# Token lists of all experts from one set of products, GpSimd's weight splits begun later, the second expert's transposes moved

## The chip, the cores and the metric

The kernel runs on one core of a Trainium2 chip. The metric is the device time of one execution in microseconds (us). The engines are TensorE (PE, matrix products, with PEld for its weight loads), VectorE (DVE), ScalarE (ACT), GpSimd (POOL), and SyncE (SP), which issues most DMAs. GpSimd issues the DMAs that gather and scatter rows by a list of indices.

## The reference, cut to what matters

The model has two layers on 512 tokens of width 1024. Each layer is a token mixer and then a mixture of 16 experts. The change lies in the expert part:

```python
g_prob = softmax(xt @ w_group + b_group);  g_val, g_idx = top_k(g_prob, 1)
e_logits = (xt @ w_expert + b_expert).reshape(N, 4, 4)      # only the chosen group's four count
e_val, e_idx = top_k(softmax(e_logits[chosen group]), 2);  e_val = e_val / sum(e_val)
gates = one_hot(g_idx * 4 + e_idx) * g_val * e_val          # two experts for each token
for e in range(16):
    hid = silu(xt @ w_gate[e]) * (xt @ w_up[e])             # 1024 -> 512
    out = out + gates[:, e:e + 1] * (hid @ w_down[e])       # 512 -> 1024
```

## The kernel before, in words

Tokens lie on 128 partitions in four tiles (`NT` = 4). Each layer first scores the tokens (`route_lt`), then `select` finds each token's group and its two best experts, in two halves of two tiles (`TS` = 2): comparisons into `beat` and `above`, the chosen group `og`, the mask `ab` of chosen experts, and a product `pk` of `ab` with a triangular matrix, which counts the earlier tokens of the same expert. `rk` (L873) is the token's place in that expert's list, or 0.

`moe` then works expert by expert on at most 96 tokens (`CAP`). `make_list(e)` (L1257) compares `rk` of expert e with the places 1 to 96 (`oneh`, L1259, DVE), and four PE matmuls with the token numbers (`pi`, L1263) give a column of 96 indices, which DVE stores (`first` L1276 for the first two experts, `lists` L1277 or L1266). GpSimd gathers the expert's rows by it (`xg`, L1278; two buffers, `XG` = 2). `gathered_t` transposes them on PE (`xt`, L521); ACT and DVE store them as a high and a low half (`th` L481, `tl` L482), since every product is made of three matmuls of halves (`mm3`, L475 to L477). `gate_up` makes `pg` and `pu`, ACT and DVE make `sg` = silu(`pg`)·`pu` (L1311, L1312), scaled by a number of `gx`; `hidden_t` transposes it (`ht`, then `hh`, `hl`); `down` makes the two halves of `pd`; ACT writes `yb` times the gate (L1343), and GpSimd scatters it with addition (`h_d` in the first layer, `out_dram` in the second, L1346). `pg` and `pu` share a PSUM tag of three buffers ("pj"), so `pu` of the second expert takes the buffer of the first expert's `pg`, which is free after the ACT step that reads it together with `gx`.

The gates take a way of their own: `rest` (L890 to L928) works out the gate values on DVE, `ga`, writes them to DRAM (`g_d`, L928), and GpSimd gathers them by each list (`gx`, L1351).

The weights of an expert are six units of 1 MB. Each comes by DMA into a `raw` buffer and is split in two pieces: ACT writes the high part (`wh`, L191), DVE or GpSimd the low one (`wl`, L193). Six pieces are held at a time. `add_moe` says whose work a low part is: GpSimd has one piece of every sixth unit (`i[0] % 6 == 3`) while the unit's number is under 60. With the order of the units (gate and up of an expert, then down of the expert before it) these are pieces of `up` for expert 0 and of `down` for the next ones. `ws.hold()` stops the weight DMAs ahead of the lists, and `ws.go` lets them on behind a mark on DVE.

The order on each engine is set by the tile framework's scheduler, from the recorded operations, their dependences and its own costs; `marks` and `behind` pin operations behind others of the same engine.

Of the kernel before, what the change touches and what calls it, by code (L numbers as in the profile page):

```python
# [15 lines left out]
F16 = mybir.dt.float16  # L16
# [8 lines left out]
P = 128  # L25
# [26 lines left out]
XG = 2  # L52
# [224 lines left out]
def tile_trunk(ctx: ExitStack, tc: tile.TileContext, x, a_norm, a_w_in, a_b_f, a_q_gain, a_k_gain, a_w_out,  # L277
# [64 lines left out]
    def add_moe(layer):  # L342
        i = [0]
        tags = RINGS[layer]

        def add4(w, r0, c0):
            ws.add([(cols(0, 512, 512), rows(w, r0, 4, c0, 512))],
                   [[(k * 1024, 1024, None, "pool" if i[0] < 60 and (i[0] % 6, k) == (3, 0) else None)] for k in range(2)],
                   tags[i[0] % len(tags)], "m")
            i[0] += 1  # L350

        def gu(e):
            for w in (moe_w_gate, moe_w_up):
                for half in range(2):
                    add4(w[layer, e], half * 512, 0)

        def down(e):
            for n in range(2):
                add4(moe_w_down[layer, e], 0, n * 512)

        gu(0)
        for e in range(1, NE):
            gu(e)
            down(e - 1)
        down(NE - 1)
# [472 lines left out]
    def select(layer, t0, t1):  # L838
# [3 lines left out]
        if t0 == 0:  # L842
            r.update(lg=kt([P, NT, 20], "lg"), beat=kt([P, NT * 5, 4, 4], "beat"),
                     above=kt([P, NT * 5, 4], "above"), og=kt([P, NT, 4], "og"), ab=kt([P, NT, NE], "ab", BF16),
                     rk=kt([P, NT, NE], "rk", F16))
        lg, ab = r["lg"], r["ab"]
# [20 lines left out]
        for t in range(t0, t1):  # L867
            o = pk[:, (t - t0) * 16:(t - t0) * 16 + 16]
            for u in range(t + 1):
# [3 lines left out]
        nc.vector.scalar_tensor_tensor(r["rk"][:, t0:t1], pk[:, 0:n * 16].rearrange("p (t e) -> p t e", e=NE), 1.0,  # L873
                                       ab[:, t0:t1], op0=ALU.add, op1=ALU.mult)

    def route(layer):
# [3 lines left out]
        lg, ab, og = r["lg"], r["ab"], r["og"]  # L880
# [10 lines left out]
        def rest():  # L891
# [7 lines left out]
            a12 = kt([P, 2, NT, NE], "a12")  # L899
            a5 = r["above"].rearrange("p (t r) e -> p t r e", r=5)  # L900
            for k in range(2):
                nc.vector.scalar_tensor_tensor(a12[:, k].rearrange("p t (g e) -> p t g e", e=4), a5[:, :, 1:5], float(k),
                                               og[:, :, :, None].to_broadcast([P, NT, 4, 4]),
                                               op0=ALU.is_equal, op1=ALU.mult)
# [330 lines left out]
    def moe(layer):  # L1235
        r = rt[layer]
        with ExitStack() as st:
# [19 lines left out]
            def make_list(e):  # L1257
                oneh = pm.tile([P, NT, CAP], F16, tag="oneh", name=f"oneh{e}", bufs=1)
                nc.vector.tensor_tensor(oneh, slot16[:, None, 0:CAP].to_broadcast([P, NT, CAP]),  # L1259
                                        rk[:, :, e:e + 1].to_broadcast([P, NT, CAP]), op=ALU.is_equal)  # L1260
                pi = ps("tr", f"pi{e}")[0:CAP]
                for t in range(NT):
                    nc.tensor.matmul(pi[:, 0:1], oneh[:, t, :], tok16[:, layer * NT + t:layer * NT + t + 1],  # L1263
                                     start=t == 0, stop=t == NT - 1)
                if e >= XG:
                    nc.vector.tensor_scalar_add(lists[:, e:e + 1], pi[:, 0:1], OOB)  # L1266
                li = lists[:, e:e + 1]
                if layer == 0 and e == NE - 1:
                    r["last"] = kt([CAP, NT], "last")
                    for t in range(NT):  # L1270

                        nc.vector.tensor_scalar(r["last"][:, t:t + 1], pi[:, 0:1], OOB + NT - t, 1.0 / NT,
                                                op0=ALU.add, op1=ALU.mult)
                if e < XG:
                    li = first[:, e:e + 1]
                    nc.vector.tensor_scalar(li, pi[:, 0:1], OOB, S - 1.0, op0=ALU.add, op1=ALU.min)  # L1276
                    nc.vector.tensor_scalar_add(lists[:, e:e + 1], pi[:, 0:1], OOB)  # L1277
                nc.gpsimd.indirect_dma_start(  # L1278
                    out=xg[e % XG], out_offset=None, in_=xn_d,
                    in_offset=bass.IndirectOffsetOnAxis(ap=li, axis=0), bounds_check=S - 1, oob_is_err=False)  # L1280
# [7 lines left out]
            def gate_up(e, th, tl):  # L1288
                pg, pu = ps("pj", f"pg{e}")[0:CAP], ps("pj", f"pu{e}")[0:CAP]
                for o in (pg, pu):  # L1290
# [12 lines left out]
                    for i in range(4):  # L1303
                        wh, wl = ws.get()
                        for j in range(2):
                            kc = i * 2 + j
                            c = slice(j * 512, j * 512 + 512)
                            mm3(o, th[:, kc, :], tl[:, kc, :], wh[:, c], wl[:, c], kc == 0, kc == KC - 1)
                sg = pm.tile([CAP, DE], F32, tag="sg", name=f"sg{e}", bufs=1)
# [45 lines left out]

            for i in range(XG):
                make_list(i)
                if i == 1:
                    ws.go(marks()[mybir.EngineType.DVE].name, last_unit[layer] + 1)
# [12 lines left out]
            make_list(2)  # L1372
# [4 lines left out]
            for e in range(NE):  # L1377
                sg = gate_up(e, *tt)
                if e + 1 < NE:
                    tt = gathered_t(e + 1)  # L1380
                if hprev is not None:
                    down(e - 1, *hprev)
                if e + 3 < NE:
                    make_list(e + 3)
# [494 lines left out]
```

## Time and profile before

| | |
|---|---|
| time, median of 3 runs | 1308.83 us (1306.35 to 1310.71) |
| profiled execution | 1309.12 us; span 1307.3 us, so 1.8 us lie around the span |
| first layer: mixer, experts | about 0 to 316 us, 316 to 626 us |
| second layer: mixer, experts | about 626 to 978 us, 978 to 1297 us |
| busy share of PE, DVE, ACT, POOL | 93%, 79%, 71%, 34% |
| mean granted TensorE clock | 0.968 of full speed |

The page gives shares over the span; the views of single stretches list instructions by start and duration, with the idle time of the engine ahead of one in brackets and what ended it. Matmuls are pipelined: one starts 0.23 us after the other though each lasts 0.39 us, so distances of starts are what counts. A GpSimd gather or scatter is listed with the time GpSimd spends on it, and the data land later.

### The profile page before, as it was taken

The numbers are of one execution on the slowest core, as the hardware profiler recorded it, in microseconds if no ns is written. First come the engines' busy times: TensorE is split into PE (matmuls) and PEld (weight loads), VectorE is DVE, ScalarE is ACT, GpSimd is POOL, SyncE is SP. The second block draws the span as 40 slices with busy tenths as digits, with TensorE's granted clock in tenths as the row PEclk, the third lists the DMA queues.
The fourth block names the chain that finished last, engine by engine and source line by source line (L and its number), as shares of the span: only waits on it lengthen the run. The fifth ranks groups of instructions, "written<-read, shape, count | busy, mean of one in ns | idle before, by whom it ended". The sixth has DMA issues, their size and how long they took to land. (4 is left out here: it accounts for less than half of the span.)

```text
span 1307.3 us, 21402 instructions
## 1 busy us (share of the span) xinstructions
PE 1218.5 (93%) x7664; PEld 1001.9 (77%) x7664; DVE 1032.8 (79%) x1882; ACT 931.8 (71%) x1697; POOL 450.3 (34%) x345
## 2 busy tenths in 40 slices
PE   8988999987898999999899999998888989999993
PEld 7987999966576777776799999998766667777762
DVE  5656798889897889998577777666698979989982
ACT  6455777565687888887477877677565868888872
POOL 3533543134564554310110101000165574446200
PEclk9999999998999999999899999999698999999997
DMA  6334232867999999993663333336569999999951
GB/s 208 84 84 99 59 77 78 271 205 259 312 349 318 346 350 359 358 359 120 194 162 94 98 90 94 114 93 212 187 217 306 318 332 369 358 341 343 344 187 17
DMA packets 166219, 286.35 MB, mean 219 GB/s; under 512 B 18346, under 2 KB 52178, under 8 KB 166104
## 3 DMA queue, kind: packets, MB, share of 16 engines
q1 hardware_dynamic: 142400, 252.03, 55.4%
q0 software_dynamic: 16688, 30.35, 10.2%
q10 hardware_dynamic: 7016, 2.49, 1.3%
q8 instruction: 65, 1.06, 0.3%
q14 instruction: 50, 0.41, 0.1%
HBM read 260.30 MB, written 21.83 MB: 216 GB/s over the span
## 5 line engine op out<-in xcount | busy, mean ns | idle before, releaser
L193 DVE TENSOR_TENSOR wl<-raw,wh 128x1024 fp32r<-128x1024 f32 (+1 forms) x388 | 475.5, 1258 | 60.1 <-ACT wh L191 58.0
L191 ACT ACTIVATE wh<-raw 128x1024 fp32r<-128x1024 f32 (+1 forms) x456 | 440.0, 989 | 76.1 <-PE pu L477 22.8
L193 POOL TENSOR_TENSOR wl<-raw,wh 128x512 fp32r<-128x512 f32 (+1 forms) x68 | 111.8, 1649 | 123.4 <-ACT wh L191 104.4
L476 PE MATMUL pj<-wl,bh 128*128 128x256 f32 x512 | 146.0, 286 | 0.0
L477 PE MATMUL pj<-wh,bl 128*128 128x256 f32 x512 | 145.8, 286 | 0.0
L475 PE MATMUL pj<-wh,bh 128*128 128x256 f32 x512 | 145.7, 286 | 0.0
L475 PE MATMUL pj<-wh,ah 128*128 128x256 f32 x384 | 112.6, 294 | 2.0 <-ACT wh L191 1.4
L476 PE MATMUL pj<-wl,ah 128*128 128x256 f32 x384 | 112.5, 293 | 1.8 <-POOL wl L193 1.8
L476 PE MATMUL pd<-wl,hh 128*96 128x512 f32 x256 | 102.4, 400 | 10.5 <-POOL wl L193 10.4
L477 PE MATMUL pj<-wh,al 128*128 128x256 f32 x384 | 111.8, 292 | 0.0
L475 PE MATMUL pd<-wh,hh 128*96 128x512 f32 x256 | 103.5, 404 | 0.0
L475 PE MATMUL pu<-wh,th 128*96 128x512 f32 x256 | 101.4, 396 | 1.7 <-issue 1.2
L476 PE MATMUL pu<-wl,th 128*96 128x512 f32 x256 | 102.4, 400 | 0.0
L477 PE MATMUL pd<-wh,hl 128*96 128x512 f32 x256 | 101.8, 399 | 0.0
L477 PE MATMUL pu<-wh,tl 128*96 128x512 f32 x256 | 101.0, 395 | 0.0
L476 PEld LDWEIGHTS pj<-wl,bh 128*128 128x128 f32 x512 | 98.0, 191 | 0.1
L475 PEld LDWEIGHTS pj<-wh,bh 128*128 128x128 f32 x512 | 97.7, 191 | 0.1
L477 PEld LDWEIGHTS pj<-wh,bl 128*128 128x128 f32 x512 | 97.8, 191 | 0.0
L1346 POOL DMA_INDIRECT out_dram<-yb,lists x16 | 49.4, 3088 | 139.6 <-ACT yb L1343 126.2
L477 PE MATMUL pg<-wh,tl 128*96 128x512 f32 x240 | 96.2, 401 | 0.0
L475 PE MATMUL pg<-wh,th 128*96 128x512 f32 x240 | 95.9, 400 | 0.0
L476 PE MATMUL pg<-wl,th 128*96 128x512 f32 x240 | 94.6, 394 | 0.0
(385 smaller groups left out, 3063.8 us busy)
## 6 DMA issues: line engine op xcount, KB each, us to landing
raw<-in_moe_w_gate_dram SPq DMA_DIRECT2D x64, 1024.0 KB
raw<-in_moe_w_up_dram SPq DMA_DIRECT2D x64, 1024.0 KB
raw<-in_moe_w_down_dram SPq DMA_DIRECT2D x64, 1024.0 KB
raw<-in_kv_w_dram SPq DMA_DIRECT2D x12, 1024.0 KB
raw<-in_a_w_in_dram SPq DMA_DIRECT2D x11, 1024.0 KB
raw<-in_b_w_q_dram SPq DMA_DIRECT2D x6, 1024.0 KB
kh<-kh POOLq DMA_DIRECT2D x24, 128.0 KB, 2.3
kl<-kl POOLq DMA_DIRECT2D x24, 128.0 KB, 2.5
```

What stands on the lines that cost most here:

```text
L191: nc.scalar.activation(hi[:, o:o + n], src, AF.Copy)
L193: e.tensor_tensor(lo[:, o:o + n], src, hi[:, o:o + n].bitcast(F32), op=ALU.subtract)
L475: nc.tensor.matmul(o, lh, rh, start=start, stop=False)
L476: nc.tensor.matmul(o, lh, rl, start=False, stop=False)
L477: nc.tensor.matmul(o, ll, rh, start=False, stop=stop)
L1346: nc.gpsimd.indirect_dma_start(out=sums[layer], out_offset=bass.IndirectOffsetOnAxis(ap=lists[:, e:e + 1], axis=0), in_=yb, in_offset=None ...
```

## The change

The lists of all 16 experts are made at once. `select` now makes for each half a one-hot tensor of the token's first and second choice (`a12`, formerly in `rest`), multiplies it by the token numbers (`mv`), and reduces `pk` to two places per token (`rs`). `make_lists` compares `rs` with the places (`oneh`, one operation for each half) and makes one product of eight matmuls of 16 columns (`pi`, a column for each expert); three kinds of copies follow (`first`, `lists`, and in the first layer `last`). `rk`, still needed elsewhere, is made in `rest`. The gathers stand alone (`gather`). GpSimd's pieces are those of units 24 to 83 in place of 0 to 59. The transposes of expert 1 go behind a mark in the middle of expert 0's `pu` in place of behind the whole of it.

```diff
-                   [[(k * 1024, 1024, None, "pool" if i[0] < 60 and (i[0] % 6, k) == (3, 0) else None)] for k in range(2)],
+                   [[(k * 1024, 1024, None, "pool" if 24 <= i[0] < 84 and (i[0] % 6, k) == (3, 0) else None)] for k in range(2)],
...
-        nc.vector.scalar_tensor_tensor(r["rk"][:, t0:t1], pk[:, 0:n * 16].rearrange("p (t e) -> p t e", e=NE), 1.0,
-                                       ab[:, t0:t1], op0=ALU.add, op1=ALU.mult)
+        for k in range(2):
+            nc.vector.scalar_tensor_tensor(a12[:, k, t0:t1].rearrange("p t (g e) -> p t g e", e=4), a5[:, :, 1:5],
+                                           float(k), og[:, :, :, None].to_broadcast([P, n, 4, 4]),
+                                           op0=ALU.is_equal, op1=ALU.mult)
+        nc.vector.tensor_tensor(r["mv"][:, :, t0:t1], a12[:, :, t0:t1],
+                                tokoob[:, None, layer * NT + t0:layer * NT + t1, None].to_broadcast([P, 2, n, NE]),
+                                op=ALU.mult)
+
+        pk = pk[:, 0:n * 16].rearrange("p (t e) -> p t e", e=NE)
+        places = beat.rearrange("p (k t) a b -> p k t (a b)", k=5)[:, 0:2]
+        for k in range(2):
+            nc.vector.scalar_tensor_tensor(places[:, k], pk, 1.0, a12[:, k, t0:t1], op0=ALU.add, op1=ALU.mult)
+        nc.vector.tensor_reduce(r["rs"][:, :, t0:t1], places, axis=AX.X, op=ALU.add)
+
+        r["pk"].append(lambda: nc.vector.tensor_tensor(r["rk"][:, t0:t1], places[:, 0], places[:, 1], op=ALU.add))
...
-            def make_list(e):
...
+            def make_lists():
+
+                oneh = pm.tile([P, 2, NT, CAP], F16, tag="sg", name="oneh", bufs=1)
+                pi = ps("tr", "pi")[0:CAP, 0:NE]
+                for t in range(0, NT, TS):
+                    shape = [P, 2, TS, CAP]
+                    nc.vector.tensor_tensor(oneh[:, :, t:t + TS], slot16[:, None, None, 0:CAP].to_broadcast(shape),
+                                            r["rs"][:, :, t:t + TS, None].to_broadcast(shape), op=ALU.is_equal)
+                for i, (t, k) in enumerate(itertools.product(range(NT), range(2))):
+                    nc.tensor.matmul(pi, oneh[:, k, t, :], r["mv"][:, k, t, :], start=i == 0, stop=i == 2 * NT - 1)
+                nc.vector.tensor_scalar(first[:, 0:XG], pi[:, 0:XG], OOB, S - 1.0, op0=ALU.add, op1=ALU.min)
+                nc.vector.tensor_scalar_add(lists, pi, OOB)
+                if layer == 0:
                     r["last"] = kt([CAP, NT], "last")
...
+            def gather(e):
                 nc.gpsimd.indirect_dma_start(
...
+                        if e == 0 and i == 2:
+                            r["mid"] = marks()[mybir.EngineType.PE]
...
+            make_lists()
             for i in range(XG):
-                make_list(i)
-                if i == 1:
-                    ws.go(marks()[mybir.EngineType.DVE].name, last_unit[layer] + 1)
+                gather(i)
+            ws.go(marks()[mybir.EngineType.DVE].name, last_unit[layer] + 1)
...
                 sg = gate_up(e, *tt)
-                if e + 1 < NE:
+                if e == 0:
+
+                    with behind({mybir.EngineType.PE: r["mid"]}):
+                        tt = gathered_t(1)
+                elif e + 1 < NE:
                     tt = gathered_t(e + 1)
                 if hprev is not None:
                     down(e - 1, *hprev)
                 if e + 3 < NE:
-                    make_list(e + 3)
+                    gather(e + 3)
                     gates(e + 3)
```

On DVE, in the first layer, this is what stood from the last `oneh` of the selection's chain to the expert's first weight splits (`wl`); `first` is the list that the first two gathers need.

```order
L1259 TENSOR_TENSOR oneh_4266<-slot_114,rk 128x384
L1276 TENSOR_SCALAR first<-pi_4268 96x1
L1277 TENSOR_SCALAR lists<-pi_4268 96x1
L1259 TENSOR_TENSOR oneh_4278<-slot_114,rk 128x384
L1276 TENSOR_SCALAR first<-pi_4280 96x1
L1277 TENSOR_SCALAR lists<-pi_4280 96x1
L902 SCALAR_TENSOR_TENSOR a_4329<-above,og 128x64 x2
L907 TENSOR_REDUCE gm<-lg 128x4
L923 COPY ga_4351<-rr_1574 128x4
L193 TENSOR_TENSOR wl_4365<-raw_3339,wh_4364 128x1024
```

In the same place there now stands this, with one `first` for both gathers:

```order
L885 SCALAR_TENSOR_TENSOR beat<-pk_2_4254,a_4172 128x32 x2
L886 TENSOR_REDUCE rs<-beat 128x2x2
L1274 TENSOR_TENSOR oneh<-slot_114,rs 128x2x192
L1278 TENSOR_SCALAR first<-pi 96x2
L1279 TENSOR_SCALAR lists<-pi 96x16
L1284 TENSOR_SCALAR last<-pi 96x1 x4
L888 TENSOR_TENSOR rk<-beat 128x32 x2
L918 TENSOR_REDUCE gm<-lg 128x4
L922 TENSOR_TENSOR sd<-a_4172 128x64
L934 COPY ga_4364<-rr_1574 128x4
L193 TENSOR_TENSOR wl_4378<-raw_3339,wh_4377 128x1024
```

The second `oneh` and `first` are gone, and two `rk`, an `sd` and, in the first layer, four `last` stand between `first` and the splits. The `oneh` of the first half stands further up, ahead of the second half's `above`.

On POOL, in the first layer, this followed the first two gathers (`xg` a gather of rows, `gx` one of gates, `h_d` a scatter, `wl` a weight split):

```order
L1278 DMA xg_4227<-xn_d,lists 96x1024
L193 TENSOR_TENSOR wl_4427<-raw_3345,wh_4426 128x1024
L1351 DMA gx_4258<-g_d,lists 96x17
L1351 DMA gx_4259<-g_d,lists 96x17
L1351 DMA gx_4260<-g_d,lists 96x17
L1278 DMA xg_4228<-xn_d,lists 96x1024
L1351 DMA gx_4261<-g_d,lists 96x17
L193 TENSOR_TENSOR wl_4615<-raw_3717,wh_4614 128x1024
L1346 DMA h_d<-yb_4655,lists 512x1024
L1278 DMA xg_4227<-xn_d,lists 96x1024
L1351 DMA gx_4258<-g_d,lists 96x17
L193 TENSOR_TENSOR wl_4799<-raw_4372,wh_4798 128x1024
```

Now it is this:

```order
L1288 DMA xg_4235<-xn_d,lists 96x1024
L1364 DMA gx_4271<-g_d,lists 96x17
L1364 DMA gx_4272<-g_d,lists 96x17
L1364 DMA gx_4273<-g_d,lists 96x17
L1364 DMA gx_4274<-g_d,lists 96x17
L1288 DMA xg_4236<-xn_d,lists 96x1024
L1288 DMA xg_4235<-xn_d,lists 96x1024
L1359 DMA h_d<-yb_4652,lists 512x1024
L1364 DMA gx_4271<-g_d,lists 96x17
L1288 DMA xg_4236<-xn_d,lists 96x1024
L1359 DMA h_d<-yb_4828,lists 512x1024
L1364 DMA gx_4272<-g_d,lists 96x17
```

No split stands between the first DMAs; the first one follows the third scatter and its `gx`. A gather of rows stands ahead of the scatter that it followed.

On PE, in the first layer, `pu1`, the second product of expert 1, followed the whole of `pg1`:

```order
L476 MATMUL pg1_4546<-wl75_4493,th1_4507 96x512
L477 MATMUL pg1_4546<-wh75_4492,tl1_4508 96x512
L475 MATMUL pu1_4547<-wh76_4548,th1_4507 96x512
L476 MATMUL pu1_4547<-wl76_4549,th1_4507 96x512
L477 MATMUL pu1_4547<-wh76_4548,tl1_4508 96x512
```

Now its first two matmuls stand behind the first two of `pg1`:

```order
L477 MATMUL pu0_4420<-wh71_4435,tl0_4398 96x512
L475 MATMUL pg1_4543<-wh72_4465,th1_4512 96x512
L476 MATMUL pg1_4543<-wl72_4466,th1_4512 96x512
L475 MATMUL pu1_4544<-wh76_4545,th1_4512 96x512
L476 MATMUL pu1_4544<-wl76_4546,th1_4512 96x512
L477 MATMUL pg1_4543<-wh72_4465,tl1_4513 96x512
```

So 22 of the 24 matmuls of `pg1` moved behind the first of `pu1`. In both layers the transposes `xt1` stand seven matmuls further ahead, inside `pu0`, and the matmuls of later lists are gone from the loop. The order on SP is unchanged, and so are the mixers.

## Rows read from the trace of the kernel before

**Rows 1.** The page: busy time of each engine, its share of the span, and its instructions.

```profile
PE 1218.5 (93%) x7664; PEld 1001.9 (77%) x7664; DVE 1032.8 (79%) x1882; ACT 931.8 (71%) x1697; POOL 450.3 (34%) x345
```

**Rows 2.** Busy time of each engine in four stretches of the first layer's expert part: start and end, busy us and instructions by engine, then the granted TensorE clock as a share of full speed, the DMA share and GB/s. The last stretch is one period of a later expert.

```profile
320.00:326.00 6.00, 4.45 (x47) 4.28 (x47) 5.22 (x15) 1.53 (x2) 4.45 (x2) 0.58 0.36 80
326.00:333.00 7.00, 6.75 (x36) 4.70 (x35) 6.73 (x21) 2.37 (x6) 5.58 (x3) 1.00 1.00 365
...
400.00:404.00 4.00, 3.45 (x9) 2.38 (x10) 1.19 (x1) 2.54 (x3) 0.49 (x1) 0.57 0.58 160
...
440.00:458.00 18.00, 18.00 (x90) 12.79 (x89) 16.35 (x18) 15.43 (x19) 8.88 (x4) 1.00 1.01 350
```

**Rows 3.** GpSimd's timeline in both layers: start, duration, what it is, and in brackets the idle time ahead of it and what ended that.

```profile
321.24 1.07 POOL L1278 DMA_INDIRECT xg<-xn_d,first  x1 [9.52 <-DVE oneh L1259]
322.62 7.88 POOL L1278 DMA_INDIRECT xg<-xn_d,first  x1 [0.30 <-DVE ga L923]
...
381.70 11.92 POOL L1346 DMA_INDIRECT h_d<-yb,lists  x1 [5.58 <-ACT yb L1343]
393.92 2.15 POOL L1278 DMA_INDIRECT xg<-xn_d,lists  x1 [0.30 <-ACT wh L191]
...
398.14 2.35 POOL L193 TENSOR_TENSOR wl<-raw,wh 128x1024 fp32r<-128x1024 f32 x1
405.68 1.60 POOL L1346 DMA_INDIRECT h_d<-yb,lists  x1 [5.18 <-ACT yb L1343]
...
983.33 1.05 POOL L1278 DMA_INDIRECT xg<-xn_d,first  x1 [9.79 <-DVE oneh L1259]
984.69 7.94 POOL L1278 DMA_INDIRECT xg<-xn_d,first  x1 [0.31 <-DVE ga L923]
```

**Rows 4.** DVE's timeline at the start of the expert part, in the first layer and (the last two rows) in the second.

```profile
319.08 0.56 DVE L1259 TENSOR_TENSOR oneh<-slot,rk 128x384 f16<-128x384 f16 x1
320.21 0.15 DVE L1276 TENSOR_SCALAR first<-pi 96x1 uint32<-96x1 f32 x1 [0.57 <-PE pi L1263]
...
321.60 0.35 DVE L902 SCALAR_TENSOR_TENSOR a<-above,og 128x64 f32<-128x64 f32 x2
...
322.02 3.49 DVE L193 TENSOR_TENSOR wl<-raw,wh 128x1024 fp32r<-128x1024 f32 x3
...
329.52 0.15 DVE L897 TENSOR_REDUCE cmax<-pc 1x1 f32<-1x16 f32 x1
...
330.28 0.53 DVE L482 TENSOR_TENSOR tl<-xt,th 128x384 fp32r<-128x384 f32 x1
...
331.29 0.55 DVE L1259 TENSOR_TENSOR oneh<-slot,rk 128x384 f16<-128x384 f16 x1
...
332.83 0.23 DVE L927 TENSOR_TENSOR ga<-a 128x64 f32<-128x64 f32 x1
...
982.33 0.15 DVE L1276 TENSOR_SCALAR first<-pi 96x1 uint32<-96x1 f32 x1 [0.57 <-PE pi L1263]
...
984.15 3.49 DVE L193 TENSOR_TENSOR wl<-raw,wh 128x1024 fp32r<-128x1024 f32 x3
```

**Rows 5.** PE's timeline from the first expert's transposes to the end of its `pd` and the list that follows, in the first layer, and four rows of the second.

```profile
325.51 0.88 PE L521 MATMUL xt<-cm,xg 96*128 96x96 f32 x8 [0.77 <-DMA xg<-xn_d,first]
...
336.91 0.85 PE L521 MATMUL xt<-cm,xg 96*128 96x96 f32 x8 [1.47 <-DMA xg<-xn_d,first]
...
348.22 0.48 PE L475 MATMUL pu<-wh,th 128*96 128x512 f32 x1 [1.24 <-issue]
...
356.08 0.48 PE L476 MATMUL pd<-wl,hh 128*96 128x512 f32 x1 [0.70 <-POOL wl L193]
357.64 0.55 PE L521 MATMUL xt<-cm,xg 96*128 96x96 f32 x4 [1.07 <-DVE hl L482]
...
362.44 0.39 PE L477 MATMUL pd<-wh,hl 128*96 128x512 f32 x1
...
362.90 0.39 PE L476 MATMUL pg<-wl,th 128*96 128x512 f32 x1
363.12 0.30 PE L1263 MATMUL pi<-tok,oneh 128*96 128x1 f16 x4
...
363.57 0.39 PE L475 MATMUL pg<-wh,th 128*96 128x512 f32 x1
...
988.17 0.88 PE L521 MATMUL xt<-cm,xg 96*128 96x96 f32 x8 [1.29 <-DMA xg<-xn_d,first]
...
999.56 0.85 PE L521 MATMUL xt<-cm,xg 96*128 96x96 f32 x8 [1.49 <-DMA xg<-xn_d,first]
...
1010.09 0.48 PE L475 MATMUL pu<-wh,th 128*96 128x512 f32 x1 [0.42 <-ACT sg L1311]
...
1024.28 0.39 PE L477 MATMUL pd<-wh,hl 128*96 128x512 f32 x1
```

**Rows 6.** PE's timeline in the third expert period of the first layer, and the row of the second layer that answers to the second one.

```profile
395.64 0.39 PE L475 MATMUL pd<-wh,hh 128*96 128x512 f32 x1
400.55 0.74 PE L476 MATMUL pd<-wl,hh 128*96 128x512 f32 x1 [4.52 <-POOL wl L193]
...
404.28 0.40 PE L477 MATMUL pd<-wh,hl 128*96 128x512 f32 x1
...
1062.38 0.74 PE L476 MATMUL pd<-wl,hh 128*96 128x512 f32 x1 [4.51 <-POOL wl L193]
```

More of the change, by code (lines that the diff above doesn't have):

```diff
@@ L844, in select @@
                      above=kt([P, NT * 5, 4], "above"), og=kt([P, NT, 4], "og"), ab=kt([P, NT, NE], "ab", BF16),
-                     rk=kt([P, NT, NE], "rk", F16))
-        lg, ab = r["lg"], r["ab"]
+                     rk=kt([P, NT, NE], "rk", F16), a12=kt([P, 2, NT, NE], "a12"), mv=kt([P, 2, NT, NE], "mv", F16),
+                     rs=kt([P, 2, NT], "rs"), pk=[])
+        lg, ab, a12 = r["lg"], r["ab"], r["a12"]
         for t in range(t0, t1):
@@ L879, in route @@
         cnt = kt([1, 1], "cnt", I32)
-        lg, ab, og = r["lg"], r["ab"], r["og"]
+        lg, ab = r["lg"], r["ab"]
         def t44(name):
@@ L898, in rest @@
             nc.vector.tensor_copy(cnt, cmax)
[L899 to L904, printed above, removed]
+            for f in r["pk"]:
+                f()
+            a12 = r["a12"]
             gl, el = lg[:, :, 0:4], lg[:, :, 4:20]
@@ L1255, in moe @@
                 nc.gpsimd.memset(v, 0.0)
-            def make_list(e):
[L1258 to L1268, printed above, removed]
+            def make_lists():
[10 more added lines that the diff above has]
+                if layer == 0:
@@ L1269, in make_list @@
                     r["last"] = kt([CAP, NT], "last")
                     for t in range(NT):
-                        nc.vector.tensor_scalar(r["last"][:, t:t + 1], pi[:, 0:1], OOB + NT - t, 1.0 / NT,
+                        nc.vector.tensor_scalar(r["last"][:, t:t + 1], pi[:, NE - 1:NE], OOB + NT - t, 1.0 / NT,
                                                 op0=ALU.add, op1=ALU.mult)
[L1274 to L1277, printed above, removed]
+            def gather(e):
@@ L1278, in make_list @@
                 nc.gpsimd.indirect_dma_start(
                     out=xg[e % XG], out_offset=None, in_=xn_d,
-                    in_offset=bass.IndirectOffsetOnAxis(ap=li, axis=0), bounds_check=S - 1, oob_is_err=False)
+                    in_offset=bass.IndirectOffsetOnAxis(ap=(first if e < XG else lists)[:, e:e + 1], axis=0),
+                    bounds_check=S - 1, oob_is_err=False)
             def gathered_t(e):
@@ L1371, in moe @@
             tt = gathered_t(0)
-            make_list(2)
+            gather(2)
             gates(2)
```

## The prediction, made blind

> **What bounds the kernel now.** I read the engine line of the page first, then the stretches, then the timelines of the stretches in which TensorE stands still. PE is busy 93% of the span [rows 1]. In a period of a later expert it is busy all of the time, 18.00 of 18, and DVE 16.35, so there only fewer matmuls help [rows 2]. What can be won or lost apart from that lies in the pauses at the start of each expert part and in its third period. One view shows each. GpSimd's timeline shows two gathers of rows at the start, the first in 1.07 us, the second in 7.88, and a scatter of 11.92 us before the split that PE's long pause waits for [rows 3]. DVE's timeline shows a run of splits without a break from 322.02 to 329.52, which covers the second gather but not the first [rows 4]. PE's timeline shows what each gather starts: transposes at 325.51 and at 336.91, and at 348.22 the first matmul of expert 1's `pu`, which needs expert 0's gates [rows 5].
>
> **The lists in the loop.** From the matmul at 362.90 to the one at 363.57 are two steps with a list between them, 0.67 us. Two steps without one take 0.46 (362.44 to 362.90, so 0.23 a step). A list costs PE 0.21. Twelve lie behind expert 0's `pd` in each layer: −2.5 us per layer [rows 5]. The `oneh` of each, 0.55 us of DVE, goes too, but DVE has 1.65 of 18 us free there, so that is worth nothing [rows 2, 4].
>
> **The third period.** PE waits for GpSimd's split, which ended only at 400.49 since the scatter, a gather and a gate gather lay ahead of it on POOL [rows 3, 6]. From 395.64 to 404.28 are 11 steps, 2.5 us at 0.23, and they take 8.6. So the pause costs 6.1 us: some 4.7 of waiting, the rest because the granted clock in 400 to 404 is 0.57, TensorE having stood still before it; part of the matmuls run at 1.2 GHz in place of 2.4 [rows 2, 6]. The idle time in the second layer is the same to 0.01 (4.51), so 6.1 there too. The change gives this split, and the two before it, to DVE: −6.1 per layer. DVE pays three splits of about 1.2 us (3.49 for three) over three periods and saves three `oneh`; I count that at nothing. If DVE were late with them, PE would wait up to 1.2 us in each.
>
> **The start.** Here the change costs. What `first` waits for gets longer: the `oneh` of the first half stands ahead of `above` now (0.56 us), and a second `beat` and the reduction `rs` come ahead of the second `oneh` (about 0.4, estimated from the four small operations between 321.60 and 322.02). The matmuls behind the last `oneh` stay four of the kind. I take `first` 1.0 us later: 321.2, and 983.3 in the second layer [rows 4]. The list of expert 1 no longer stands between `first` and the splits; in its place are ten small operations in the first layer, six in the second, at 0.08 to 0.1 each. So the run of splits begins 0.8 to 1.0 us behind `first` in the first layer and 0.5 to 0.6 in the second. Gather 0 began 1.03 and 1.00 us behind it (321.24 against 320.21, 983.33 against 982.33) [rows 3, 4]. It now begins just inside the run, where so far only gather 1 did.
>
> What a gather that begins there does is on record twice: 7.88 and 7.94 us, until 0.98 us after the run ended (322.62 + 7.88 = 330.50, against 329.52) [rows 3, 4]. Every instruction of the run reads two inputs from SBUF. The Trainium skill (SBUF — State Buffer, Who interferes with whom) says that a DVE instruction with two SBUF inputs gets in the way of GpSimd's reads, but infers that `tensor_tensor` does not hold up the making of DMA descriptors, which needs the write side. By that rule gather 0 would pass as before, which is the first rival below; the trace speaks against it with the two gathers of 7.9 us, and I go by the trace.
>
> The run is as long as before without its `oneh` (7.5 − 0.5 = 7.0), so it ends near 329.1 and 990.9, and gather 0 at 330.1 and 991.9. Its data then meet the weight loads. Gather 0 took 3.2 us from its end to the transposes (322.31 to 325.51) while the DMA share was 0.36, gather 1 took 6.4 with the share at 1.00; in the second layer 3.8 and 6.9 [rows 2, 3, 5]. I take the later ones, the loads being the same: transposes of expert 0 at 336.5 in place of 325.51, and at 998.8 in place of 988.17. The other end is 3.2 and 3.1 us earlier.
>
> From there two chains lead to expert 1's `pu`. One is PE's own: 8 transposes, 24 `pg`, 24 `pu`, 8 transposes, 2 `pg`, so 50 steps of 0.23 and two times 0.85, 0.3 for ACT, and 1.4 for the low clock after 11 us of standing still (the 6.1 less 4.7 of above): 15.0 us. The other is the gates': DVE's second `tl` 1.1 us behind the transposes' start, 2.0 to `ga` (330.28 to 332.83 less the list and `oneh` between), then 15.4 from `ga` to `pu` (332.83 to 348.22): 18.5. Of this the write of the gates met a queue with loads; in the held case DVE frees no weight buffer from 329 to 340, the loads run dry, and I take off the difference of the two landings, 3.2: 15.3. So `pu` starts at 336.5 + 15.3 = 351.8 and at 1014.1, not at 348.22 and 1010.09.
>
> Behind it more is left to do than before. From 348.22 to 362.44 were 14.2 us, with 1.8 idle for GpSimd's late split and `hl`, which fall away with GpSimd's split; 22 matmuls of `pg` come to stand there, 5.1: 17.5 [rows 5]. The last `pd` of expert 0 starts at 369.3 (before 362.44, +6.9) and 1031.6 (before 1024.28, +7.3). Moving expert 1's transposes into expert 0's `pu` saves nothing of its own in this case: gather 1, now at the run's end behind gather 0, lands a little after it and well before it is wanted, and the pause at 336.91 is within the sum.
>
> **Sum.** First layer 6.9 − 6.1 − 2.5 = −1.7, second 7.3 − 6.1 − 2.5 = −1.3: −3.0. The profiled execution took 1309.12, 0.3 more than the median, and the 1.8 us around the span stay: 1306.1 on its scale, 1305.8 beside the median of 1308.83. With gather 0 landing early in both layers it is 1299.5; with the gates' chain at its full 18.5 in both, 1312.2. This is the likeliest case's own range. GpSimd's ten splits go to later units; they cost nothing there as long as they keep ahead of PE, as in the period shown, where PE has no idle time [rows 2].
>
> **Rivals.**
> Gather 0 passes. In the first layer the gather and the run begin within 0.2 us of each other, and gather 0 of before ran its last 0.3 us beside a split unharmed. For it speaks that margin; against it the second layer, where the run is 0.4 ahead. By the rule of the Trainium skill cited above (SBUF — State Buffer) this would hold in both layers. Then PE has its transposes about 1 us late, gather 1 is held as now, and the gates bound `pu`: `ga` at 329.1 + 3.3 less 0.5 for the `oneh` = 331.9, `pu` at 347.3, `pd` 17.5 later plus 1.4 for a low clock, as PE runs out of work some 8 us ahead: 366.2, +3.8 in place of +6.9. The second layer gains some 0.5 more. In both layers: 1299 beside the median; in the first alone, 1302.7.
>
> The late split comes back (slower). The first of GpSimd's splits now stands behind the third scatter and a gate gather. In before it was the second scatter that took 11.92 us under a run of DVE splits; the third took 1.60, but after a pause of PE's [rows 3]. Without the pause, and with all splits of three experts on DVE, the run may last longer. Between the scatter's start and PE's need were 14.2 us (381.70 to 395.9); from the end of the gather at 396.07 to that of the split at 400.49, with the gate gather between, went 4.4. So a scatter of over 9.8 us makes PE wait again, and each such pause costs up to 6.1: 1312 with one, 1318 with one in each layer. Against it: in the later period shown GpSimd has splits behind scatters too, and PE never waits [rows 2].
>
> The change doesn't remove the pause: DVE has 16.35 of 18 us taken in a period; with GpSimd's split and without the list it is 17.0 [rows 2]. Should it start the second period behind PE, it has little to catch up with and PE waits for it, 1 to 3 us in each layer. That gives 1308 to 1312. Against it: GpSimd's splits no longer lie beside DVE's.
>
> **How the numbers follow.** Chances: gather 0 held in both layers with no late split 0.52, passing in one or both 0.26, a late split back 0.14, DVE late in its place 0.08. Forecast: 1305.8 us. About 3.9 us, 0.3%, is what can be told from no change here. The first case lies at −3.0 with ends at −9.3 and +3.4: some 0.42 of it faster, 0.52 the same, 0.06 slower; the second is faster in 0.85 and else the same; the third slower in 0.85; the fourth the same in 0.55, slower in 0.3. That gives faster 0.45, same 0.37, slower 0.18. The range from 1296.5 to 1314.5 takes in both landings, the passing gather in both layers with 2 us to spare, and one late split.
>
> **What would show it.** Right: gather 0 lists 7 to 8 us in both layers; PE is idle about 11 us ahead of the first transposes; `pu` of expert 1 starts near 352 and 1014; the third period takes under 18.5 us; later periods are 17.7 apart. Wrong: a gather 0 of about 1 us, a PE row of several us of idle time ended by POOL's `wl` in the fourth or fifth period, or `pd` of expert 0 ending as early as before.

## The result, and the profile after

The changed kernel takes 1317.35 us in the median (1314.31 to 1319.27, 15 runs), the kernel before, on the same chip, 1305.91 (1297.26 to 1312.10, 15 runs). The ratio is 1.0102, 95% interval 1.008 to 1.0125: slower by 11.4 us between the medians and by some 13 by the ratio, where 3 us less were forecast, and beyond the range's end of 1314.5. The profiled execution took 1315.84 us (span 1314.1), 6.7 more than that of before. Two differences have to be explained, then: +6.7 in place of −3.0 between two profiles, and +13 between the runs.

The page's engine line of the kernel after shows that PE and DVE have less to do (against [rows 1]). POOL has the same 345 instructions, and its splits take 111.3 us after 111.8; nearly all of what it lost, 450.3 to 382.4, is time listed for gathers and scatters (221.6 to 154.1):

```profile
PE 1215.7 (93%) x7552; PEld 999.2 (76%) x7552; DVE 1016.3 (77%) x1842; ACT 930.9 (71%) x1697; POOL 382.4 (29%) x345
```

GpSimd's timeline of the kernel after, with the same columns as [rows 3]: the first two gathers of both layers, the first gate gather and the second scatter.

```profile
319.02 7.91 POOL L1288 DMA_INDIRECT xg<-xn_d,first  x1 [10.43 <-DVE ga L934]
327.24 0.99 POOL L1288 DMA_INDIRECT xg<-xn_d,first  x1 [0.30 <-issue]
...
340.91 0.97 POOL L1364 DMA_INDIRECT gx<-g_d,lists  x1 [4.39 <-DMA g_d<-ga]
...
389.52 1.61 POOL L1359 DMA_INDIRECT h_d<-yb,lists  x1 [5.11 <-ACT yb L1356]
...
986.34 7.67 POOL L1288 DMA_INDIRECT xg<-xn_d,first  x1 [10.71 <-DVE ga L934]
994.32 1.00 POOL L1288 DMA_INDIRECT xg<-xn_d,first  x1 [0.30 <-issue]
```

Before, gather 0 listed 1.07 and gather 1 7.88; now it is the other way round, in both layers. DVE's timeline after says why (the rows that answer to [rows 4]): the run of splits begins at 318.88, 0.14 us ahead of gather 0, and ends at 325.92; the gather ends at 326.93.

```profile
317.98 0.15 DVE L1278 TENSOR_SCALAR first<-pi 96x2 uint32<-96x2 f32 x1 [0.58 <-PE pi L1277]
...
318.88 2.35 DVE L193 TENSOR_TENSOR wl<-raw,wh 128x1024 fp32r<-128x1024 f32 x2
...
325.92 0.15 DVE L911 TENSOR_REDUCE cmax<-pc 1x1 f32<-1x16 f32 x1
...
335.21 0.56 DVE L482 TENSOR_TENSOR tl<-xt,th 128x384 fp32r<-128x384 f32 x1 [9.07 <-ACT th L481]
...
337.51 0.23 DVE L938 TENSOR_TENSOR ga<-a 128x64 f32<-128x64 f32 x1
```

PE's timeline after, to be laid beside [rows 5]: expert 0's transposes, the first matmul of expert 1's `pu`, and expert 0's last `pd`, in both layers.

```profile
333.75 1.54 PE L521 MATMUL xt<-cm,xg 96*128 96x96 f32 x8 [12.59 <-DMA xg<-xn_d,first]
...
351.92 0.74 PE L475 MATMUL pu<-wh,th 128*96 128x512 f32 x1 [2.61 <-ACT sg L1324]
...
370.42 0.39 PE L477 MATMUL pd<-wh,hl 128*96 128x512 f32 x1
...
1000.85 1.54 PE L521 MATMUL xt<-cm,xg 96*128 96x96 f32 x8 [12.24 <-DMA xg<-xn_d,first]
...
1019.89 0.47 PE L475 MATMUL pu<-wh,th 128*96 128x512 f32 x1 [2.61 <-ACT sg L1324]
...
1038.55 0.39 PE L477 MATMUL pd<-wh,hl 128*96 128x512 f32 x1
```

PE stands still for 12.6 and 12.2 us ahead of the transposes, and again for 2.6 ahead of `pu`, which waits for ACT's `sg`. ACT's timeline after shows what lay ahead of that `sg`:

```profile
341.42 6.75 ACT L191 ACTIVATE wh<-raw 128x1024 fp32r<-128x1024 f32 x7 [5.29 <-PE pg L1312]
348.07 0.84 ACT L481 ACTIVATE th<-xt 128x384 fp32r<-128x384 f32 x2
348.81 1.05 ACT L191 ACTIVATE wh<-raw 128x1024 fp32r<-128x1024 f32 x1
349.88 1.28 ACT L1324 ACT_TABLE_LOAD   x1
351.18 0.68 ACT L1324 ACTIVATE sg<-pg,gx 96x512 f32<-96x512 f32 x1
```

`sg` follows there without a wait. In ACT's timeline of the kernel before the table was loaded early enough, and `sg` did wait for the gates, as the prediction had it:

```profile
341.66 1.28 ACT L1311 ACT_TABLE_LOAD   x1
347.48 0.68 ACT L1311 ACTIVATE sg<-pg,gx 96x512 f32<-96x512 f32 x1 [4.54 <-DMA gx<-g_d,lists]
```

The view of stretches after, with the columns of [rows 2]: PE's long wait, the two stretches at a lower granted clock behind the two pauses, and a later period.

```profile
327.00:334.00 7.00, 0.25 (x2) 0.25 (x3) 0.00 (x0) 0.00 (x0) 0.99 (x1) 0.50 1.04 298
334.00:341.00 7.00, 7.00 (x28) 4.95 (x28) 2.38 (x12) 1.19 (x3) 1.04 (x2) 0.72 0.35 90
...
348.00:355.00 7.00, 4.27 (x12) 2.33 (x11) 5.27 (x7) 4.00 (x7) 1.11 (x1) 0.76 0.97 316
440.00:458.00 18.00, 18.00 (x87) 12.74 (x86) 16.21 (x16) 15.54 (x19) 7.00 (x4) 1.00 1.02 340
```

One measure for all profiles, since the mixers' length varies by itself (span less both expert parts: 692 to 704 us, with the same code): PE's timeline from the first matmul of the second half's rank products (`pk`, 318.53 and 980.66 in the kernel before) to the layer's last `pd`. All times count from there, first layer / second layer. The last column is for kernels that were timed in rounds.

| kernel | transposes of expert 0 | expert 0's last `pd` | third period | expert part | ratio to before, 95% |
|---|---|---|---|---|---|
| before | 6.98 / 7.51 | 43.90 / 43.62 | 23.98 / 24.12 | 306.05 / 305.93 | 1 |
| after | 17.80 / 17.55 | 54.48 / 55.25 | 17.69 / 17.69 | 308.77 / 309.49 | 1.0102 [1.008, 1.0125] |
| e1 | 7.71 / 7.52 | 44.11 / 44.68 | 17.70 / 17.72 | 298.73 / 298.64 | 0.9943 [0.9916, 0.997] |
| e2 | 7.49 / 7.55 | 57.45 / 55.95 | 17.69 / 17.69 | 310.66 / 309.14 | 1.0121 [1.006, 1.0182] |
| e3 | 17.77 / 17.67 | 54.10 / 53.11 | 17.69 / 17.69 | 315.19 / 307.40 | 1.0117 [1.0058, 1.0175] |
| e4 | 6.98 / 6.80 | 48.46 / 47.27 | 17.90 / 17.91 | 305.42 / 304.22 | 1.0017 [0.9982, 1.0052] |
| e5 | 7.77 / 7.45 | 52.35 / 52.03 | 17.68 / 17.69 | 306.52 / 305.88 | 1.0051 [1.0017, 1.0086] |
| e6 | 7.71 / 7.31 | 43.83 / 42.89 | 17.68 / 17.68 | 297.71 / 297.00 | 0.9932 [0.9899, 0.9964] |
| e7 | 18.27 / 16.88 | 56.47 / 55.19 | 17.72 / 17.72 | 310.31 / 309.06 | |
| e8 | 17.90 / 17.70 | 56.49 / 55.53 | 17.69 / 17.69 | 311.21 / 310.03 | |
| e9 | 7.19 / 6.99 | 43.03 / 43.00 | 17.91 / 17.91 | 304.80 / 302.44 | 1.004 [1.0005, 1.0074] |
| e10 | 17.78 / 18.11 | 54.53 / 54.65 | 17.46 / 17.46 | 309.23 / 309.12 | 1.0119 [1.0034, 1.0204] |
| e11 | 7.06 / 6.84 | 48.61 / 46.62 | 17.89 / 17.87 | 308.01 / 305.89 | |
| e12, before | 6.99 / 6.78 | 43.31 / 42.25 | 17.88 / 24.60 | 299.32 / 305.39 | |
| e13 | 7.11 / 6.72 | 41.51 / 42.91 | 17.88 / 17.89 | 309.78 / 309.63 | 1.0018 [0.9973, 1.0063] |
| e14, before | 6.88 / 6.88 | 43.19 / 43.11 | 17.88 / 24.61 | 299.25 / 306.71 | |
| e15, before | 6.97 / 7.49 | 43.04 / 40.92 | 17.88 / 23.89 | 299.01 / 302.95 | |
| e16, before | 7.13 / 6.97 | 43.88 / 40.65 | 17.88 / 24.61 | 299.90 / 304.22 | |

### The profile page after: what moved, and what is told of

The parts are those of the page before. It is cut to its first block, busy times and chain, and to the rows that moved or that the text cites. A ratio compares the mean times of both kernels' runs of the same rounds, so it can differ in the third digit from the quotient of the medians.

```text
span 1314.1 us, 21168 instructions
## 1 busy us (share of the span) xinstructions
PE 1215.7 (93%) x7552; PEld 999.2 (76%) x7552; DVE 1016.3 (77%) x1842; ACT 930.9 (71%) x1697; POOL 382.4 (29%) x345
## 5 line engine op out<-in xcount | busy, mean ns | idle before, releaser
L193 POOL TENSOR_TENSOR wl<-raw,wh 128x512 fp32r<-128x512 f32 (+1 forms) x68 | 111.3, 1642 | 188.8 <-ACT wh L191 179.0
L475 PE MATMUL pj<-wh,ah 128*128 128x256 f32 x384 | 111.8, 292 | 0.6 <-DVE y L492 0.6
L196 DVE SCALAR_TENSOR_TENSOR wl<-raw,gcols,wh 128x256 fp32r<-128x256 f32 x144 | 63.9, 482 | 21.2 <-ACT wh L195 21.0
```

The costliest lines, as they stand in the source:

```text
L193: e.tensor_tensor(lo[:, o:o + n], src, hi[:, o:o + n].bitcast(F32), op=ALU.subtract)
L196: nc.vector.scalar_tensor_tensor(lo[:, o:o + n], src, gain, hi[:, o:o + n].bitcast(F32), op0=ALU.mult, op1=ALU.subtract)
L475: nc.tensor.matmul(o, lh, rh, start=start, stop=False)
```

## The experiments

All of them compute the whole output.

**e1: the splits behind the gates' working-out.** The changed kernel with one line: the mark that holds back DVE's first splits is set behind `rest`.

```diff
+            dve = marks()[mybir.EngineType.DVE]
```

> The changed kernel with its first weight splits on DVE placed behind the whole working-out of the gates, so that no split runs while gather 0 is being made. Theory A (the cost of the change is that gather 0 is held by the run of splits): gather 0 lists about 1 us in place of 7.9, expert 0's transposes start about 7 us behind the second half's rank products in place of 17.7, expert 0's last down product ends 38 to 41 us behind them in place of 54.4, and the time is 1284 to 1293 us. Theory B (the cost lies in the longer chain up to the list and in the moved place of expert 1's second product): the transposes come earlier, but the time falls by less than 8 us, to 1309 or more.

1297.64 us (1294.89 to 1299.03), ratio 0.9943 [0.9916, 0.997]: faster than both kernels. GpSimd's timeline of e1:

```profile
320.80 1.11 POOL L1288 DMA_INDIRECT xg<-xn_d,first  x1 [10.41 <-DVE ga L934]
322.21 0.99 POOL L1288 DMA_INDIRECT xg<-xn_d,first  x1 [0.30 <-issue]
...
331.11 0.97 POOL L1364 DMA_INDIRECT gx<-g_d,lists  x1 [0.30 <-issue]
```

With small operations on DVE in place of splits both gathers pass, and the gates are gathered 11.6 us earlier (13.4 against 25.0 us behind the rank products). Expert 0's last `pd` comes at 44.11 in place of 54.48, about where the kernel before has it, so the whole cost of the change lies at the start, and one line takes it away. The line does two things, it frees the gather and it puts the gates early; e1 alone doesn't tell them apart. The gain behind it, 254.6 us from expert 0's last `pd` to the end against 254.3, is untouched. Theory A's 38 to 41 us and 1284 to 1293 were too low: PE still waits 2.4 us for the first gather's data and 2.1 for `th`.

**e2 and e5: a wait for gather 0.** The splits wait for a small operation of GpSimd's behind gather 0. In e2 the scheduler then laid the gates' operations among the later splits; in e5 the order on DVE, PE and POOL is that of the changed kernel, but for a `tl` on DVE and a group of `ht` on PE; on ACT one `wh` moves ahead of the exponential `e`.

```diff
+                if i == 0:
+                    with behind({pool.engine: pool}):
+                        nc.gpsimd.memset(done[:, 0:1], 0.0)
...
+            nc.vector.tensor_copy(done[:, 1:2], done[:, 0:1])
```

> The changed kernel in which the DVE splits wait until GpSimd has made gather 0 (a tiny fill on GpSimd behind the gather, read by DVE ahead of the splits). The scheduler lays the gates' chain among the next splits here. Theory A: gather 0 lists about 1 us, expert 0's transposes start about 8 us behind the rank products, PE's idle 12.7 us goes; the gates then bound expert 1's second product at about 36 us, so that expert 0's last down product ends near 49 us in place of 54.4, and the time is 1302 to 1309. Theory B: no gain over the changed kernel beyond 3 us, 1314 to 1319.

> As the experiment in which the splits wait for gather 0, but with the gates' chain kept ahead of the seventh split, so that DVE, PE and GpSimd keep the order of the changed kernel; only the hold of gather 0 is gone. Theory A (the hold is the cost): transposes of expert 0 about 7.5 us behind the rank products in place of 17.7, DVE's low halves at about 13 in place of 20.5, all that follows 7 to 8 us earlier, expert 0's last down product at 46 to 48, time 1300 to 1305 us. Theory C (the end of expert 0 is set by ACT's run of splits or by the gates whatever gather 0 does): that product at 52 or later, 1313 or more.

Gather 0 lists 1.07 us in both, and the transposes come 10 us earlier. Yet e2 takes 1321.06 us and e5 1309.52 (1.0051 [1.0017, 1.0086]). The start gained was lost again ahead of expert 1's `pu`: PE waits there 10.9 us in e2 (first layer) and 8.6 in e5. ACT's timeline of e5:

```profile
336.60 1.06 ACT L192 ACTIVATE wh<-raw 128x1024 fp32r<-128x1024 f32 x1 [6.60 <-PE pg L1317]
337.56 0.19 ACT L931 ACTIVATE e<-d 128x4 f32<-128x4 f32 x1
...
352.39 0.68 ACT L1329 ACTIVATE sg<-pg,gx 96x512 f32<-96x512 f32 x1 [5.96 <-DMA gx<-g_d,lists]
```

GpSimd's gather of the gates in e5, and PE's wait for `sg`:

```profile
343.76 4.13 POOL L1369 DMA_INDIRECT gx<-g_d,lists  x1 [10.78 <-DMA g_d<-ga]
```

```profile
353.13 0.74 PE L480 MATMUL pu<-wh,th 128*96 128x512 f32 x1 [8.56 <-ACT sg L1329]
```

The exponential `e`, on which the gates depend, stands on ACT behind a `wh` that waits 6.6 us for a free buffer. So the gates are late, their gather falls under DVE's next run, and `sg` waits for it. Neither theory's number came true in full: with gather 0 free and the gates late, 2 to 3 us per layer are won (52.35 against 54.48, 52.03 against 55.25), not 10. e1, which has the gates early too, gets the other 7 to 8. What gather 0 is worth by itself, with the gates no later than in the changed kernel, no run shows.

**e3: `pu` of expert 1 behind the whole of `pg`,** in the changed kernel.

```diff
+                        with behind({pe.engine: pe} if e == 1 and o is pu else {}):
```

> The changed kernel with expert 1's second product put behind the whole of its first one again, on PE alone. Gather 0 stays held. Theory A: only the 3.0 us that PE waits for the gates at the start of that product go in each layer, so 1310 to 1313. Theory B (the moved place is the cost): 1303 or less.

1320.70 us, against both theories; ratio 1.0117 [1.0058, 1.0175], not to be told from the changed kernel's. So the order is not the cost. PE waits all the same, 1.8 us inside `pg` for DVE's `tl`, which stands behind seven splits. Expert 0's last `pd` came 0.4 and 2.1 us earlier; a period of 24.74 at the end of the first layer ate more than that in the profile: a scatter held for 9.60 us there made ACT, and then PE, late.

**e4, e11 and e10: each part alone.** e4 is the kernel before with GpSimd's splits at units 24 to 83; e11 the kernel before with the moved transposes; e10 the changed kernel with both undone, that is, the merged lists alone.

```diff
-                   "pool" if i[0] < 60 and (i[0] % 6, k) == (3, 0) else None
+                   "pool" if 24 <= i[0] < 84 and (i[0] % 6, k) == (3, 0) else None
...
+                        if e == 0 and i == 2:
+                            r["mid"] = marks()[mybir.EngineType.PE]
```

> The kernel before with GpSimd's splits moved to units 24 to 83 and nothing else. If the pause in the third period comes from GpSimd's late split alone: the period falls from 24.0 to about 17.9 us in both layers, and the time by 12 to 16 us, to 0.988 to 0.991 of before. If DVE is late in its place: the period stays above 20 us and the time within 5 us of before.

> The kernel before with expert 1's transposes moved into expert 0's pu, nothing else. Theory A (the move saves nothing of its own: the held second gather lands too late for it, and PE then waits for it at the earlier place): expert 0's last pd 43.3 to 45 us behind the rank products, third period 24 as before. Theory B (it is worth a wait of PE ahead of the transposes): 1 us or more less, 42.9 or below. Theory C (the wait at the earlier place costs): 45 or above.

> The merged lists alone: GpSimd's splits at their old units and expert 1's transposes at their old place. Theory A (the lists alone bring both the cost and the gain): first gather held 7 to 8 us, transposes of expert 0 17 to 18.5 us behind the rank products, its last pd at 54.5 to 57, third period under 18.5 in both layers, from expert 0's last pd to the end 253.5 to 255; ratio to before 1.007 to 1.014. Theory B (the other two parts carry some of either): the third period back at 22 to 24, or the last pd of expert 0 under 52; ratio outside 1.007 to 1.014.

e10 has it all: gather 0 at 7.91 us, expert 0's last `pd` at 54.5 and 54.7, no long third period, ratio 1.0119. GpSimd's timeline of e10:

```profile
321.75 7.91 POOL L1288 DMA_INDIRECT xg<-xn_d,first  x1 [10.40 <-DVE ga L934]
```

So the lists carry both the cost and the gain, as theory A had it. e4 makes no difference that can be measured, where 12 to 16 us less were expected if the late split alone made the pause: it too has no period of 24 us, but pays 4 us at the start (`pu` waits 3.5 us for `sg`) and one period of 19.7. e11 missed its theory A: the transposes in the middle of `pu` cost 3 to 5 us in the kernel before, because `pu` of expert 1 then waits 5.1 us in the first layer and 2.6 in the second for `sg`, and that one, in the first layer's ACT rows, for the gates. Its third period is 17.9, with old lists and old splits, and the fourth 20.6. Two profiles of one run each, e11's and e8's below, are all there is on this part.

**e7 and e8: one part undone.** The changed kernel with GpSimd's splits at units 0 to 59 (e7), and with the transposes at their old place (e8).

> The changed kernel with GpSimd's splits at units 0 to 59 again. Gather 0 stays held (transposes 17.7 us behind the rank products). Theory A: the third period is 24 us again (the second scatter held, the split late), and expert 0's last down product comes 1 to 2 us earlier than 54.5, since GpSimd takes two of its splits: 8 to 10 us more than the changed kernel, 1324 to 1328. If the lists' removal had ended the pause by itself: period under 18.5 and 1312 to 1317.

> The changed kernel with expert 1's transposes behind the whole of expert 0's second product again. All theories: gather 1 lands well ahead of either place, so the move is worth little: expert 0's last down product within 1.5 us of 54.5, time 1315 to 1320. A larger change would show that the moved transposes, or the order that the scheduler makes around them, are part of the cost.

e7 took 1314.69 us, e8 1320.65, one run each. In e8 expert 0's last `pd` comes 2.0 and 0.3 us later than in the changed kernel, where at most 1.5 were expected; one run can't show whether the place of the transposes is worth anything. In e7 the long third period did not return. GpSimd's timeline of e7, in that period:

```profile
391.40 8.92 POOL L1359 DMA_INDIRECT h_d<-yb,lists  x1 [4.97 <-ACT yb L1356]
400.62 1.03 POOL L1364 DMA_INDIRECT gx<-g_d,lists  x1 [0.30 <-issue]
401.68 2.43 POOL L193 TENSOR_TENSOR wl<-raw,wh 128x1024 fp32r<-128x1024 f32 x1
404.27 1.78 POOL L1288 DMA_INDIRECT xg<-xn_d,lists  x1 [0.16 <-issue]
```

With the old splits, GpSimd's order is now scatter, gate gather, split, gather of rows. The gather of rows no longer stands between scatter and split, and PE does not wait for the split though the scatter is held. So the merged lists are enough to take the pause away, without the later splits; they are not the only thing that does, as e4 and e11 show.

**e6: e1 with the table of `silu` loaded early.** One more line, a `silu` of four columns behind the exponentials.

```diff
+            nc.scalar.activation(kt([P, 4], "junk"), e2, AF.Silu)
```

> The kernel of the first experiment with a tiny silu behind the gates' exponentials on ACT, which loads the table of silu while ACT stands still, in place of behind six weight splits. If ACT's row of splits, table and silu is what expert 1 waits for there (PE idle 2.1 us ahead of its first product, ended by ACT's high halves), 1.3 to 2.8 us per layer go: 1292 to 1296 us. If gather 1 or the weights bound it, less than 1 us: 1296 to 1299.

1293.39 us (1291.23 to 1297.42), ratio 0.9932 [0.9899, 0.9964]: the lowest ratio of this study, though its interval and e1's overlap widely. The expert parts of the profile are 1.0 and 1.6 us shorter than e1's. The load of 1.28 us moved from the stretch ahead of `sg` to 318.50, where ACT was idle.

**e9: the line of e1 in the kernel before.**

> The kernel before with the one line of the first experiment: DVE's run of splits goes behind the working-out of the gates, so that the second gather lists about 1 us and the gates are written early. Theory A (the gathers and the gates at the start are worth something in both kernels, the change brought the shorter periods): the second gather of rows lists 1.0 to 1.2 us, expert 0's last pd starts 40 to 43 us behind the rank products (43.9 and 43.6 before), from there to the layer's last pd 262 as before, with the 24 us period still in it; 1298 to 1304, ratio 0.994 to 0.999. Theory B (the freed gathers pay only because the change had held them back, the kernel before had nothing to win there): 43.5 to 45 behind the rank products, ratio 0.999 to 1.003.

Ratio 1.004 [1.0005, 1.0074], against both theories. The second gather lists 0.99 us, and expert 0's last `pd` is 0.6 to 0.9 us earlier than in the first profile of before; but three periods in the first layer and two in the second are 19.6 long, where PE waits 1.4 us or so for GpSimd's split behind a held scatter. In the kernel before the line wins nothing; with the change it is worth 1.6%.

**e12 to e16: the kernel before, again, and with one split taken from GpSimd.** e12, e14, e15 and e16 are the kernel before. In e13 the split that PE waits for in the third period goes to DVE.

```diff
-                   "pool" if i[0] < 60 and (i[0] % 6, k) == (3, 0) else None
+                   "pool" if i[0] < 60 and i[0] != 21 and (i[0] % 6, k) == (3, 0) else None
```

> The kernel before once more, for a second profile. What lies outside the two expert parts (span less the two stretches from the rank products to the last pd) was 692 to 704 us in the profiles so far, with the same code: it should again lie there, and need not be 695.4; the two expert parts should be 306.0 each to within 0.7 us, with the period of 24 us in each.

> The kernel before, with one split per layer (the one that TensorE's pause in the third period waits for) given from GpSimd to DVE, one more row on DVE and one less on GpSimd in each layer, all other orders the same. Theory A (the pause comes in some executions and not in others, and is what spreads the times of before from 1292 to 1312): third period 17.8 to 19 us in both layers, expert 0's last pd at 42 to 44 us behind the rank products as before, runs within 7 us of each other at about 1291 to 1299, ratio 0.993 to 0.997. Theory B (the pause only moves: the held scatter makes the next split or DVE late): a stall of 2 us or more in the third or fourth period, ratio 0.998 to 1.003, times spread as before. Theory C (the spread of before has another cause, in the mixers): no pause, but times still spread over 15 us or more.

> The kernel before, a third profile. Theory A: each third period is either about 17.9 or about 24 us, nothing between, and the time is near 1293 to 1298 with no period of 24, 1300 to 1305 with one, 1306 to 1312 with two. Theory C: the time does not follow the number of long periods.

> The kernel before, a fourth profile: as for the third. Theory A: 1293 to 1298 us with no period of 24, 1300 to 1305 with one, 1306 to 1312 with two. Theory C: no such order.

> The kernel before, a fifth profile: as for the third. Theory A: 1293 to 1298 us with no period of 24, 1300 to 1305 with one, 1306 to 1312 with two. Theory C: no such order.

In all four new profiles the long third period is there in the second layer and not in the first, which then takes 299.0 to 299.9 us in place of 306.05. They took 1303.95, 1305.12, 1302.83 and 1300.43 us, the first one, with two long periods, 1309.12. That is close to theory A's times, with one execution alone that has two long periods and none without. GpSimd's timeline of e12, the first two scatters of the first layer and of the second:

```profile
361.32 1.98 POOL L1346 DMA_INDIRECT h_d<-yb,lists  x1 [8.27 <-ACT yb L1343]
...
379.04 2.08 POOL L1346 DMA_INDIRECT h_d<-yb,lists  x1 [7.62 <-ACT yb L1343]
...
1019.66 5.04 POOL L1346 DMA_INDIRECT out_dram<-yb,lists  x1 [7.96 <-ACT yb L1343]
...
1037.38 11.88 POOL L1346 DMA_INDIRECT out_dram<-yb,lists  x1 [5.62 <-ACT yb L1343]
```

In the ten layers of the five profiles there are only these two courses: first scatter 2.0, second 2.1, no pause (four layers), or first 5.0 to 5.1, second 11.9, and the pause (six). e13 shows that the pause is not bound to its split. GpSimd's timeline of e13, and the row of PE that waits, in a later period:

```profile
375.72 14.63 POOL L1346 DMA_INDIRECT h_d<-yb,lists  x1 [5.58 <-ACT yb L1343]
...
416.05 13.23 POOL L1346 DMA_INDIRECT h_d<-yb,lists  x1 [4.25 <-ACT yb L1343]
...
432.69 2.35 POOL L193 TENSOR_TENSOR wl<-raw,wh 128x1024 fp32r<-128x1024 f32 x1
```

```profile
435.09 0.74 PE L476 MATMUL pd<-wl,hh 128*96 128x512 f32 x1 [4.72 <-POOL wl L193]
```

Its scatters are held all the same and stalls come one and two periods later; its runs spread from 1297 to 1318, ratio 1.0018 [0.9973, 1.0063]. That is theory B for the pause, with a spread somewhat wider than before's (1292.87 to 1311.54 in the same rounds). What stays open is which small difference at the start decides between the two courses, and whether runs near 1292 have no long period at all; none such was profiled.

## Why the prediction was wrong

**The start, up to the transposes: right.** Gather 0 listed 7.91 and 7.67 us, to 1.01 us behind the run's end. The transposes began 17.80 and 17.55 us behind the rank products, where 336.5 and 998.8 would be 18.0 and 18.1. The rule of the Trainium skill (SBUF — State Buffer, Who interferes with whom) by which the gather would have passed does not agree with this trace; e1, with the run away, has it at 1.11. What it is in the run that holds the gather, no run shows.

**The start, from the transposes to `pu`: the step that failed.** The "two chains" were 15.0 and 15.3; measured were 18.17 and 19.04 (351.92 − 333.75, 1019.89 − 1000.85). The gates were not what was late: their gather began at 340.91, some 10 us ahead of `sg`, and the queue was as quiet as forecast (DMA share 0.35). A third chain, ACT's own, was not counted. With DVE and the loads run dry, ACT's seven `wh` wait until PE frees a weight buffer, at 341.4. They take 6.75 us; `th`, another `wh` and the table load, 3.1 together, come before `sg`. So PE stood still for 2.61 us ahead of `pu`, in both layers. That chain is read from the rows; no run shortened it in the changed kernel by itself. PE's own chain, without that wait, took 15.56 and 16.43 us for the 15.0: the term for the low clock, 1.4, was too small in the second layer, where the clock was 0.58 in 1001 to 1008 (0.72 in 334 to 341). Behind `pu`, the 17.5 became 18.5 and 18.66, with the granted clock at 0.76 in 348 to 355, behind a pause of 2.6 us that the sum did not have. Expert 0's last `pd` came 3.7 and 4.3 us later than the forecast's 50.8 and 50.9.

**The gains: nearly right between these two profiles.** From expert 0's last `pd` to the end: −7.85 and −8.06, for −8.6. The third period gave −6.3 and −6.4 (−6.1 forecast); the lists gave 1.6 of 2.5: a period is shorter by 0.18, not 0.21, and one, the twelfth, is 0.5 longer. 3.7 + 4.3 + 0.8 + 0.5 is 9.3 of the 9.7 us between −3.0 and +6.7.

**The third period as a certainty: the other failed step.** "The change gives this split, and the two before it, to DVE: −6.1 per layer" took one profile's pause as always there, since both layers showed it alike. The later profiles have it in the second layer alone. In their first layers the way from expert 0's last `pd` to the end is 256.0 us, so against these the change wins 1.7, not 8. So the typical kernel before is faster than the one profiled, and the change has 6 us less to win. The table bears this out: the two expert parts of before, mean of five profiles, are 605.7 us together, after 618.3, so +12.5, against 13.3 by the ratio (10.4 to 16.3). The same sum gives −8.4 for e1 (measured −7.4), −11.0 for e6 (−8.9) and +6.7 for e5 (+6.6). It fails for e13, +13.7 against a measured +2.3; the execution profiled there took 1314.01, 6 us over its kernel's median. Nor was the split's new owner needed: e7 and e10 lose the pause with the old splits. The forecast's base was high as well: the median was 1308.83 in three runs and 1305.91 in fifteen.

**The rivals.** Gather 0 did not pass. No late split came back: the scatters of the kernel after take 1.4 to 2.0 us. DVE was not late. The slower side was given to the wrong mechanism.

## What to carry to other kernels

Before pricing a pause that a change will remove, look at two or three profiles of the same kernel: a pause that hangs on a held transfer may be there in one execution and gone in the next. When a transfer is late, follow every engine that then runs dry, not only the two chains that were longest before: here ACT's queue, refilled only as PE freed buffers, became the longest. And put short work that others wait for (a gather's start, the gates) ahead of a long unbroken run: one line did that here, and turned 1.0% slower into 0.6% faster.

## What the runs showed of the hardware

A GpSimd gather that takes 1.0 to 1.1 us by itself took 7.7 to 7.9 when it began 0.1 to 0.6 us inside a run of DVE's two-input operations, and ended 1 us behind the run's end (kernels before and after). Scatters, of 1.4 to 2.1 us in the kernel after and in most periods of the kernel before, took up to 14.6 (e13). In five profiles of the kernel before a layer took one of two courses in its first periods, 6 to 7 us apart, and the two layers of one execution need not take the same.
